# Four edits around the seams of a two-layer trunk: order of the expert stages' head, the last expert's rows by products, the tail LayerNorms on other engines

## The chip, the cores and the metric

The kernel runs on 1 core of one Trainium2 chip. The metric is the device time in microseconds (us) of one execution.

## The reference

A trunk of two layers over 512 tokens of width 1024, all in float32. Layer 0 mixes tokens by RWKV-7, layer 1 by forgetting attention (FoX). After each mixer comes a mixture of 16 experts with one router shared by both layers (top-1 group of four, in it top-2 experts). Each residual step is a LayerNorm with gain and shift:

```python
h = layer_norm(ALPHA * h + mixed, ln_g[i, 0], ln_b[i, 0])
ffn = shared_router_moe(h, router_w, router_bias, w_gate[i], w_up[i], w_down[i])
h = layer_norm(ALPHA * h + ffn, ln_g[i, 1], ln_b[i, 1])
```

For each token the experts give silu(x @ w_gate) * (x @ w_up) @ w_down, weighted by the two gates, which are scaled to a sum of one.

## The kernel before, in words

The stages run one after another: rwkv, moe for layer 0, fox (which begins with the LayerNorm that closes layer 0), moe for layer 1, and the last LayerNorm with the stores (trunk). Tokens lie in four tiles of 128. Products in full precision are made from two-part operands: ScalarE rounds a matrix to its high part (wsplitA, L200), VectorE subtracts to get the low part (wsplitB, L203), and three TensorE products (mm3, L68 to L70) add up.

Inside moe and between the stages the order on each engine is the order of the program text, and each engine takes its own queue in order. Inside rwkv, fox and the last LayerNorm a planner (Threads) interleaves generators: each yields estimated costs per engine, and the one whose time is least goes on; what it emits is again a fixed order on each engine.

*Head of an expert stage* (moe, from L193). From the router's sums VectorE works out the chosen experts in small operations (L209 to L231), TensorE counts positions, one-hot masks give the rows of the first expert, and GpSimd gathers them from the stored tokens hd (L253: 128 rows for experts 0 and 1; L262: half rows for the second block of up to 64 tokens). Then VectorE splits weight 0 (loA), works out codes, gate sums and the records of a table (L391 to L408) and the gate parts gp of expert 0 (L411 to L414), GpSimd scatters the table (L423), the tokens are transposed and split (xposeT, xposeS, xposeB; L280, L64, L65, L310), and VectorE splits weights 1 to 5. The first dense products are those of the second block (more(0), L314); in its middle a gate product (gates0, L419) needs gp, and VectorE copies its result (L420).

*Experts.* For each expert: more(e) if over 128 tokens chose it, then expert(e), which also splits the weights of the next one; each low part's subtraction lets SP load the weight eight places on. The expert's rows are added to the tokens zd in DRAM by an indirect DMA on GpSimd (scatter, L339). ORDER fixes which expert comes when. After the last expert there is a branch (L441) for experts with over 192 tokens.

*Closing LayerNorm* (Combine). It loads the sums z from zd (load_z, L467); in layer 0 the gain and shift rows are spread over the partitions by one-row products (spread, L462) and ScalarE copies (L465). For each tile ln_steps (L140): statistics, mean and variance on VectorE (L123 to L131), the square root and the normalisation on ScalarE (L126, L135), and gain and shift in halves on VectorE or GpSimd, whichever the planner has free sooner (L148). In the end each tile is stored whole (L1333).

*Tail of a mixer.* The last output products end in residual sums by halves (in fox L1254), the same ln_steps runs for each tile (After.norm), and the router transposes and multiplies the normalised tokens (L154, L159). Loads of the first weights start as buffers come free.

## Time and profile before

| | |
|---|---|
| time, median of 3 runs | 1638.11 us (1634.1 to 1641.88) |
| the profiled execution's own time | 1635.95 us |
| its span, first to last instruction | 1634.2 us |
| mean granted TensorE clock | 0.921 |
| TensorE busy | 1459.5 us (89%) |
| VectorE busy | 1163.1 us (71%) |
| ScalarE busy | 919.5 us (56%) |
| GpSimd busy | 530.7 us (32%) |

The profile names engines PE (TensorE products), PEld (its weight loads), DVE (VectorE), ACT (ScalarE), POOL (GpSimd) and SP (SyncE, which issues DMAs). L12 is line 12 of the kernel. A timeline row has start, duration, engine, line, operation, output and inputs by the program's names, shape and how many were merged; in brackets the idle time before and what ended it. A row of the windows view has the stretch, its length, the busy time and number of instructions that touch it for each engine, then the granted TensorE clock as a share of full speed, the DMA engines' busy share and GB/s.

### The profile page before, as it was taken

Reading aid. Unit: us, or ns where it says so; the run is one execution under the profiler, and the core shown is the slowest. Engines: PE = TensorE matmul, PEld = TensorE weight load, DVE = VectorE, ACT = ScalarE, POOL = GpSimd, SP = SyncE. Lnnn points to the kernel's source line nnn. Section 1 sums busy time; section 2 is a strip of 40 time slices with the busy share of each in tenths; the row PEclk is TensorE's granted clock in tenths of the full one; section 3 lists DMA queues with packets and bytes.
Section 4 is the critical chain, followed back from the end, with each engine's and each line's share of the span. In section 5 each row is a group of like instructions: output and inputs, shape, how many; then the busy total and the mean of one; then the engine's idle time right before and its main releaser. Section 6 shows DMA issues by size and latency. Waiting matters only on the chain. (4 is left out here: it accounts for less than half of the span.)

```text
span 1634.2 us, 24892 instructions
## 1 busy us (share of the span) xinstructions
PE 1459.5 (89%) x9125; PEld 1192.7 (73%) x9125; DVE 1163.1 (71%) x1873; ACT 919.5 (56%) x1355; POOL 530.7 (32%) x431
## 2 busy tenths in 40 slices
PE   6998977889976799999999699999885999999992
PEld 2587865887765688888887577777674888888881
DVE  7647779477585796887895637556647786968984
ACT  2553573534334486767885436545424786858872
POOL 4104785413242433322342323101104233313422
PEclk9998998587987899999999799999995999999996
DMA  7325532133345799897992424112427797979962
GB/s 221 123 84 187 162 99 83 27 98 117 111 142 189 239 331 316 287 358 232 357 344 94 157 72 123 37 61 72 155 104 227 244 364 247 358 249 346 350 204 106
DMA packets 202521, 313.61 MB, mean 192 GB/s; under 512 B 27914, under 2 KB 123490, under 8 KB 202356
## 3 DMA queue, kind: packets, MB, share of 16 engines
q1 hardware_dynamic: 178820, 267.74, 48.1%
q0 software_dynamic: 18816, 37.31, 8.0%
q10 hardware_dynamic: 4720, 6.44, 1.1%
q8 instruction: 93, 1.52, 0.4%
q14 instruction: 72, 0.59, 0.1%
HBM read 296.42 MB, written 41.75 MB: 207 GB/s over the span
## 5 line engine op out<-in xcount | busy, mean ns | idle before, releaser
L203 DVE TENSOR_TENSOR wl<-raw,wh 128x2048 fp32r<-128x2048 f32 (+1 forms) x168 | 334.7, 2006 | 5.9 <-DVEq L344 5.9
L200 ACT ACTIVATE wh<-raw 128x2048 fp32r<-128x2048 f32 (+1 forms) x168 | 282.7, 1688 | 15.7 <-ACT wh L200 9.0
L339 POOL DMA_INDIRECT zd<-yt,TB x38 | 113.7, 2992 | 432.2 <-ACT yt L306 386.0
L68 PE MATMUL bank<-wh,xm 128*128 128x256 f32 (+1 forms) x768 | 249.9, 325 | 3.9
L69 PE MATMUL bank<-wl,xm 128*128 128x256 f32 (+1 forms) x768 | 245.1, 319 | 0.0
L70 PE MATMUL bank<-wh,xm 128*128 128x256 f32 (+1 forms) x768 | 244.9, 319 | 0.0
L68 PEld LDWEIGHTS bank<-wh,xm 128*128 128x128 f32 x768 | 144.6, 188 | 26.0 <-issue 14.6
L69 PEld LDWEIGHTS bank<-wl,xm 128*128 128x128 f32 x768 | 144.7, 188 | 11.5
L70 PEld LDWEIGHTS bank<-wh,xm 128*128 128x128 f32 x768 | 144.6, 188 | 11.3
L203 DVE TENSOR_TENSOR wl<-rawo,wh 128x2048 fp32r<-128x2048 f32 (+1 forms) x56 | 110.2, 1980 | 24.9 <-ACT wh L200 24.4
L68 PE MATMUL bank<-wh,wh 128*128 128x512 f32 x256 | 111.5, 436 | 1.4 <-DVE kl L1169 0.8
L68 PE MATMUL bank<-wh,hm 128*128 128x512 f32 x256 | 111.3, 435 | 0.0
L70 PE MATMUL bank<-wh,wl 128*128 128x512 f32 x256 | 101.1, 395 | 3.6 <-DVE wl L1240 3.6
L70 PE MATMUL bank<-wh,hm 128*128 128x512 f32 x256 | 101.1, 395 | 0.0
L69 PE MATMUL bank<-wl,hm 128*128 128x512 f32 x256 | 100.8, 394 | 0.0
L200 ACT ACTIVATE wh<-rawo 128x2048 fp32r<-128x2048 f32 (+1 forms) x56 | 93.4, 1668 | 13.1 <-PE bank L70 9.0
L69 PE MATMUL bank<-wl,wh 128*128 128x512 f32 x256 | 100.6, 393 | 0.0
L1062 POOL TENSOR_TENSOR wl<-raw,wh 128x512 fp32r<-128x512 f32 x29 | 41.2, 1432 | 88.6 <-ACT wh L1061 87.0
L262 POOL DMA_INDIRECT xo<-hd,TB x30 | 61.1, 2037 | 11.9 <-issue 8.6
L64 ACT ACTIVATE xm<-bank 128x512 fp32r<-128x512 f32 x64 | 38.3, 598 | 42.5 <-PE bank L280 38.9
L68 PEld LDWEIGHTS bank<-wh,wh 128*128 128x128 f32 x256 | 49.2, 192 | 15.1 <-issue 6.0
L1197 ACT ACTIVATE sb<-sb,st 128x512 f32<-128x512 f32 (+1 forms) x64 | 35.8, 560 | 43.2 <-DVE st L1193 27.3
(531 smaller groups left out, 3504.1 us busy)
## 6 DMA issues: line engine op xcount, KB each, us to landing
raw<-in_moe_w_gate_dram SPq DMA_DIRECT2D x48, 1024.0 KB
raw<-in_moe_w_up_dram SPq DMA_DIRECT2D x48, 1024.0 KB
raw<-in_moe_w_down_dram SPq DMA_DIRECT2D x48, 1024.0 KB
rawo<-in_moe_w_up_dram SPq DMA_DIRECT2D x16, 1024.0 KB
rawo<-in_moe_w_down_dram SPq DMA_DIRECT2D x16, 1024.0 KB
rawo<-in_moe_w_gate_dram SPq DMA_DIRECT2D x14, 1024.0 KB
raw<-in_fx_w_in_dram SPq DMA_DIRECT2D x12, 1024.0 KB
raw<-in_rw_wk_dram SPq DMA_DIRECT2D x4, 1024.0 KB
```

The source lines that it names most:

```text
L64: nc.scalar.activation(hi,src,AF.Copy)
L68: nc.tensor.matmul(out,ah,bh,start=start,stop=False)
L69: nc.tensor.matmul(out,ah,bl,start=False,stop=False)
L70: nc.tensor.matmul(out,al,bh,start=False,stop=stop)
L200: Q=slice(None) if q is None else QS[q]; nc.scalar.activation(his[m%NH][:,Q],raws[m%NR][:,Q],AF.Copy)
L203: Q=slice(None) if q is None else QS[q]; V.tensor_tensor(los[m%NH][:,Q],raws[m%NR][:,Q],his[m%NH][:,Q].bitcast(F32),op=ALU.subtract)
L262: nc.gpsimd.indirect_dma_start(out=xo,out_offset=None,in_=hd.rearrange("t (h n) -> (t h) n",h=2), in_offset=bass.IndirectOffsetOnAxis(ap=T ...
L339: nc.gpsimd.indirect_dma_start(out=zd[:,:],out_offset=bass.IndirectOffsetOnAxis(ap=ix[0:n],axis=0), in_=y[0:n],in_offset=None,bounds_check ...
L1062: (V if d else G).tensor_tensor(lo[n][:,Q],raw[:,Q],hi[n][:,Q].bitcast(F32),op=ALU.subtract)
L1197: S.activation(SB[u][:,0:N],SB[u][:,0:N],AF.Exp,bias=ST[u][:,0:1],scale=-1.0,accum_out=ST[u][:,1:2])
```

## The change

- **Order of the head.** The codes go ahead of the split of weight 0; table records, code sums and gate sums go from VectorE to GpSimd as chains of small additions (total); a mask of the first choice (thr1) replaces the running sums of choices; the token transposes and all splits of weights come ahead of the gate parts gp. In layer 1 the first two weights are split in fox already (pre=2, t_early, the end of t_last).
- **The last expert's rows by products.** Expert 15 scatters nothing. z is loaded before it; a one-hot matrix hot of its rows against tokens is made, and after the branch Combine.sums adds, for each tile and half, identity times z and hot times the expert's output y in a PSUM bank: 16 products in fp32. The LayerNorm reads the banks. In layer 0 the gain and shift rows are spread inside expert 15.
- **LayerNorm.** ln_quick does everything but the square root on VectorE, two combined passes for each half. It is used for the last tile of both mixers and for tiles 2 and 3 of the last LayerNorm; tiles 0 and 1 there have gain and shift on GpSimd alone. The last stores are of half tiles.

```diff
+def ln_quick(C, th, z, i, out, gb, bb, mark, eps=LN_EPS, keys=()):
+    V=C.nc.vector; sm=C.sm[:,i%4]; N=(slice(0,512),slice(512,1024)); z=halves(z)
+    for n in range(2):
+        yield from th.need(*keys[n:n+1])
+        V.bn_stats(sm[:,6*n:6*n+6],z[n]); yield 'V',.69
+    V.bn_aggr(sm[:,12:14],sm[:,0:12].rearrange("p (a b) -> p a b",a=2))
+    V.tensor_scalar(sm[:,14:15],sm[:,13:14],eps,None,op0=ALU.add)
+    C.nc.scalar.activation(sm[:,15:16],sm[:,14:15],AF.Sqrt)
+    sub=lambda n: V.scalar_tensor_tensor(out[:,N[n]],z[n],sm[:,12:13],gb[:,N[n]],op0=ALU.subtract,op1=ALU.mult)
+    sub(0); V.reciprocal(sm[:,14:15],sm[:,15:16]); yield 'V',1.2
+    for n in range(2):
+        if n: sub(1)
+        V.scalar_tensor_tensor(out[:,N[n]],out[:,N[n]],sm[:,14:15],bb[:,N[n]],op0=ALU.mult,op1=ALU.add); yield 'V',.69*(n+1)
+        mark(n)
...
-        for m in range(NH): wsplitA(m)
+        for m in range(pre,NH): wsplitA(m)
...
+        G=nc.gpsimd; mk=su[:,384:512].rearrange("p (c t e) -> p c t e",c=2,e=NE); m0=mk[:,0].rearrange("p t (g e) -> p (t g) e",g=4)
+        V.tensor_tensor(m0,rk,C.thr1[:,None,:].to_broadcast([128,16,4]),op=ALU.is_lt)
+        G.tensor_tensor(m0,m0,gs.rearrange("p t g -> p (t g)")[:,:,None].to_broadcast([128,16,4]),op=ALU.mult)
+        G.tensor_tensor(mk[:,1],selb,mk[:,0],op=ALU.subtract)
...
         first(0)
+        mt=sTs[0].rearrange("p a b -> p (a b)").rearrange("p (c t e) -> p c t e",c=2,e=NE); red=p1.tile([128,3,8],F32,name="red"); idx=p1.tile([128,8],I32,name="idx")
+        mt2=sTs[1].rearrange("p a b -> p (a b)").rearrange("p (c t e) -> p c t e",c=2,e=NE)
+        ct=lambda t: t.rearrange("p c t e -> p (c t) e"); bc=lambda t: t[:,None,:,:].to_broadcast([128,2,NT,NE])
+        def total(out, t):
+            t=ct(t)
+            for n in (8,4,2): G.tensor_tensor(t[:,:,0:n],t[:,:,0:n],t[:,:,n:2*n],op=ALU.add)
+            G.tensor_tensor(out,t[:,:,0],t[:,:,1],op=ALU.add)
+        G.tensor_tensor(mt2,mk,bc(s),op=ALU.mult); total(red[:,1],mt2)
+        G.tensor_tensor(red[:,2,0:4],red[:,1,0:4],red[:,1,4:8],op=ALU.add)
...
-        loA(0); V.tensor_copy(sel,selb)
+        bl=su[:,256:320].rearrange("p (a b) -> p a b",b=NE); code=su[:,320:384].rearrange("p (a b) -> p a b",b=NE); pos=pp[:,0:NT,:]
+        V.tensor_scalar(bl,pos,127.5,None,op0=ALU.is_gt)
+        for n in (255.5,383.5): V.scalar_tensor_tensor(bl,pos,n,bl,op0=ALU.is_gt,op1=ALU.add)
+        V.scalar_tensor_tensor(code,pos,64.0,C.e4[:,None,:].to_broadcast([128,NT,NE]),op0=ALU.mult,op1=ALU.add)
+        V.scalar_tensor_tensor(code,bl,-8191.0,code,op0=ALU.mult,op1=ALU.add)
+        V.reciprocal(red[:,2,0:4],red[:,2,0:4]); V.tensor_scalar(red[:,2,0:4],red[:,2,0:4],1.0/ALPHA,None,op0=ALU.mult)
+        for m in range(pre): load(m+NR)
...
+            if not next_: comb.spread((pgo,tr[1]),0)
...
+            if not next_: comb.spread((pgo,tr[1]),2)
...
-            lo(4); dnA(w[5],5,1); outA(1,y,fo); scatter(src(e),y,128); hi(5); lo(5)
+            lo(4); dnA(w[5],5,1); outA(1,y,fo)
+            if next_: scatter(src(e),y,128)
+            hi(5); lo(5)
...
-        bl=su[:,256:320].rearrange("p (a b) -> p a b",b=NE); code=su[:,320:384].rearrange("p (a b) -> p a b",b=NE); pos=pp[:,0:NT,:]
-        V.tensor_scalar(bl,pos,127.5,None,op0=ALU.is_gt)
-        for n in (255.5,383.5): V.scalar_tensor_tensor(bl,pos,n,bl,op0=ALU.is_gt,op1=ALU.add)
-        V.scalar_tensor_tensor(code,pos,64.0,C.e4[:,None,:].to_broadcast([128,NT,NE]),op0=ALU.mult,op1=ALU.add)
-        V.scalar_tensor_tensor(code,bl,-8191.0,code,op0=ALU.mult,op1=ALU.add)
-        mk=su[:,384:512].rearrange("p (c t e) -> p c t e",c=2,e=NE); m1=mk[:,1].rearrange("p t (g e) -> p (t g) e",g=4)
-        V.memset(m1[:,:,0],0.0); V.tensor_copy(m1[:,:,1],selv[:,:,0])
-        V.tensor_tensor(m1[:,:,2],selv[:,:,0],selv[:,:,1],op=ALU.add)
-        V.tensor_tensor(m1[:,:,3],m1[:,:,2],selv[:,:,2],op=ALU.add)
-        V.tensor_tensor(mk[:,1],mk[:,1],sel,op=ALU.mult)
-        V.tensor_tensor(mk[:,0],sel,mk[:,1],op=ALU.subtract)
-        mt=sTs[0].rearrange("p a b -> p (a b)").rearrange("p (c t e) -> p c t e",c=2,e=NE); red=p1.tile([128,3,8],F32,name="red"); idx=p1.tile([128,8],I32,name="idx")
-        ct=lambda t: t.rearrange("p c t e -> p (c t) e"); bc=lambda t: t[:,None,:,:].to_broadcast([128,2,NT,NE])
-        V.tensor_tensor(mt,mk,bc(code),op=ALU.mult)
-        V.tensor_reduce(red[:,0,:,None],ct(mt),axis=AX.X,op=ALU.add); V.tensor_copy(idx,red[:,0])
-        V.tensor_tensor(mt,mk,bc(s),op=ALU.mult)
-        V.tensor_reduce(red[:,1,:,None],ct(mt),axis=AX.X,op=ALU.add)
-        V.tensor_tensor(red[:,2,0:4],red[:,1,0:4],red[:,1,4:8],op=ALU.add); V.reciprocal(red[:,2,0:4],red[:,2,0:4]); V.tensor_scalar(red[:,2,0:4],red[:,2,0:4],1.0/ALPHA,None,op0=ALU.mult)
-        V.tensor_tensor(C.rec[:,:,2].rearrange("p (c t) -> p c t",c=2).bitcast(F32),red[:,1].rearrange("p (c t) -> p c t",c=2),red[:,2:3,0:4].to_broadcast([128,2,NT]),op=ALU.mult)
+        if not pre: loA(0)
+        for hf in range(2): xposeT(xgs[0],hf,tr[hf]); xposeS(hf,tr[hf])
+        if not pre: loA(1)
+        xposeB()
+        for m in range(2,NH): loA(m)
+        G.tensor_tensor(mt,mk,bc(code),op=ALU.mult); total(red[:,0],mt)
+        G.tensor_copy(idx,red[:,0])
+        G.tensor_tensor(C.rec[:,:,2].rearrange("p (c t) -> p c t",c=2).bitcast(F32),red[:,1].rearrange("p (c t) -> p c t",c=2),red[:,2:3,0:4].to_broadcast([128,2,NT]),op=ALU.mult)
         g0=p1.tile([128,2],F32,name="g0"); gp=p1.tile([128,3,NT],BF16,name="gp"); gr=p1.tile([128,NT],F32,name="gr")
         V.tensor_tensor(gr,s[:,:,ORDER[0]],red[:,2,0:4],op=ALU.mult)
...
-        for hf in range(2): xposeT(xgs[0],hf,tr[hf]); xposeS(hf,tr[hf])
-        loA(1); xposeB()
-        for m in range(2,NH): loA(m)
         for e in range(NE):
             count(e+2)
             more(e)
             if e+2<NE or e==0: gather(src(2) if e==0 else src(e+2),xgs[e%2],128)
             if e+1<NE: gather2(e+1)
+            else:
+                comb.load_z(); hot,tok=xgs[0][:,0:512],xgs[0][:,512:1024]; me=p1.tile([128,1],F32,name="me")
+                nc.gpsimd.iota(tok,pattern=[[1,T]],base=0,channel_multiplier=0,allow_small_or_imprecise_dtypes=True)
+                V.tensor_copy(me,src(e)); V.tensor_scalar(hot,tok,me,None,op0=ALU.is_equal)
             expert(e)
         with tc.If(nc.values_load(most[0:1,0:1],min_val=0,max_val=T,skip_runtime_bounds_check_because="a count of 512 tokens")>192):
@@ -443,12 +475,14 @@
                 count(e)
                 for blk in (1,2,3):
                     with tc.If(rs[e]>max(192,128*blk)): rest(e,blk)
+            comb.load_z()
+        comb.sums(hot,ys[1])
...
+    def spread(s, banks, a):
+        if s.rows:
+            C=s.C
+            for n in (0,1): C.nc.tensor.matmul(banks[n],s.bb[0:1,896:1024],C.raws[3][0:1,(a+n)*512:(a+n+1)*512],start=True,stop=True)
+            for n in (0,1): C.nc.scalar.activation(C.raws[2][:,(a+n)*512:(a+n+1)*512],banks[n],AF.Copy)
...
+    def sums(s, hot, y):
+        for i in range(NT):
+            for n in range(2):
+                N=slice(n*512,(n+1)*512); mm=s.C.nc.tensor.matmul
+                mm(s.C.bk[2*i+n],s.C.ident,s.h[i][:,N],start=True,stop=False,skip_group_check=True)
+                mm(s.C.bk[2*i+n],hot[:,i*128:(i+1)*128],y[:,N],start=False,stop=True,skip_group_check=True)
...
+    def steps(s, i, th, how='', mark=lambda n: None):
+        C=s.C; z,out=C.bk[2*i:2*i+2],s.h[i]
+        if how=='Q': yield from ln_quick(C,th,z,i,out,s.gb,s.bb,mark,eps=LN_EPS/ALPHA**2); return
+        if how=='G':
+            ln_stats(C,z,i,LN_EPS/ALPHA**2); ln_scale(C,i); yield 'V',2.0
+            ln_norm(C,z,i,out); yield 's',1.6
+            for n in range(2):
+                N=slice(n*512,(n+1)*512); G=C.nc.gpsimd
+                G.tensor_tensor(out[:,N],out[:,N],s.gb[:,N],op=ALU.mult); G.tensor_tensor(out[:,N],out[:,N],s.bb[:,N],op=ALU.add); mark(n)
+            return
+        yield from ln_steps(s.C,th,s.C.bk[2*i:2*i+2],i,s.h[i],s.gb,s.bb,eps=LN_EPS/ALPHA**2)
...
-    comb.load_z(); comb.spread(); comb.spread2()
...
+        if i<NT-1: yield from need(f"r{i}0",f"r{i}1")
+        yield from after.norm(i,z[i],th,z[i],(f"r{i}0",f"r{i}1"))
+        if i==NT-1: after.lo(0,1); after.lo(1)
+    def t_early():
+        yield from need(f"r{NT-1}0")
+        yield .8
+        after.hi(0,0); yield 'S',.95
+        after.lo(0,0); yield 'v',1.15
+        after.hi(0,1); after.hi(1); yield 'S',2.9
...
+        if i==NT-1: yield from ln_quick(s.C,th,z,i,out,s.gb,s.bb,mark,keys=keys)
+        else: yield from ln_steps(s.C,th,z,i,out,s.gb,s.bb,mark)
...
-        moe(C,1,W,hd[1],zd[1],load[1],0)
-        cb[1].load_z()
+        moe(C,1,W,hd[1],zd[1],cb[1],load[1],0,pre=2)
         th=Threads()
         def last(i):
-            yield 2.0*i
-            yield from cb[1].steps(i,th)
-            nc.sync.dma_start(out[0,i*128:(i+1)*128,:],cb[1].h[i])
+            yield 2.1*i
+            N=lambda n: slice(n*512,(n+1)*512)
+            yield from cb[1].steps(i,th,'GGQQ'[i],lambda n: nc.sync.dma_start(out[0,i*128:(i+1)*128,N(n)],cb[1].h[i][:,N(n)]))
```

## Rows read from the trace of the kernel before

**Rows 1.** The page's head, busy time of each engine over the span.
```profile
PE 1459.5 (89%) x9125; PEld 1192.7 (73%) x9125; DVE 1163.1 (71%) x1873; ACT 919.5 (56%) x1355; POOL 530.7 (32%) x431
```

**Rows 2.** Windows view, a stretch inside the second expert stage.
```profile
1550.00:1602.00 52.00, 51.70 (x310) 44.60 (x308) 38.18 (x36) 32.51 (x36) 14.32 (x6) 1.00 0.54 177
```

**Rows 3.** Timeline, the last tile's LayerNorm at the end of fox.
```profile
1221.09 1.28 DVE L123 BATCH_NORM_STATS2 sm<-raw 128x6 f32<-128x512 f32 x2
...
1224.31 2.75 DVE L148 TENSOR_TENSOR raw<-raw,raw 128x512 f32<-128x512 f32 x4 [0.88 <-ACT raw L135]
...
1225.78 1.11 PE L154 MATMUL bank<-ident,raw 128*128 128x128 f32 x4 [5.33 <-DVE raw L148]
```

**Rows 4.** Timeline, the head of layer 0's expert stage.
```profile
530.54 2.29 DVE L203 TENSOR_TENSOR wl<-raw,wh 128x2048 fp32r<-128x2048 f32 x1
...
535.36 0.60 ACT L64 ACTIVATE xm<-bank 128x512 fp32r<-128x512 f32 x1 [2.53 <-DMA rawo<-in_moe_w_gate_dram]
...
537.02 0.15 DVE L411 TENSOR_TENSOR gr<-s,red 128x4 f32<-128x4 f32 x1
...
538.09 1.28 DVE L65 TENSOR_TENSOR xm<-bank,xm 128x512 fp32r<-128x512 f32 x2
...
542.01 0.77 PE L314 MATMUL bank<-wh,xh 128*128 128x512 f32 x1 [2.06 <-issue]
...
542.71 8.95 DVE L203 TENSOR_TENSOR wl<-raw,wh 128x2048 fp32r<-128x2048 f32 x4
...
547.71 0.45 PE L419 MATMUL bank<-gp,yt 128*128 128x1 bf16 x12
```

**Rows 5.** Windows view, the stretches in which the clock rose, both heads.
```profile
546.00:547.00 1.00, 1.00 (x5) 0.84 (x4) 1.00 (x1) 0.00 (x0) 0.79 (x1) 0.91 0.92 118
...
1259.00:1260.00 1.00, 1.00 (x5) 0.76 (x3) 1.00 (x1) 0.00 (x0) 0.78 (x1) 0.72 0.97 242
```

**Rows 6.** Timeline, the head of layer 1's expert stage.
```profile
1253.71 0.76 PE L314 MATMUL bank<-wh,xh 128*128 128x512 f32 x1 [2.11 <-DVE xh L65]
...
1254.38 8.95 DVE L203 TENSOR_TENSOR wl<-raw,wh 128x2048 fp32r<-128x2048 f32 x4
...
1260.17 0.45 PE L419 MATMUL bank<-gp,yt 128*128 128x1 bf16 x12
```

**Rows 7.** Timeline, a small operation on GpSimd at the start of fox.
```profile
898.72 0.28 POOL L1035 CAST idb<-ident 128x128 bf16<-128x128 f32 x1
```

**Rows 8.** Timeline, from the last expert of layer 0 into fox.
```profile
889.77 0.60 ACT L306 ACTIVATE yt<-bank 128x512 f32<-128x512 f32 x1 [0.80 <-PE bank L70]
...
892.85 5.75 PE L462 MATMUL bank<-raw,raw 1*128 1x512 f32 x8 [3.12 <-ACTq L441]
...
896.93 0.60 ACT L465 ACTIVATE raw<-bank 128x512 f32<-128x512 f32 x1 [1.11 <-PE bank L462]
...
898.64 0.60 ACT L465 ACTIVATE raw<-bank 128x512 f32<-128x512 f32 x1 [1.11 <-PE bank L462]
...
901.05 1.29 DVE L123 BATCH_NORM_STATS2 sm<-raw 128x6 f32<-128x512 f32 x2 [14.63 <-DMA raw<-zd]
...
914.59 3.45 PE L1051 MATMUL bank<-ident,raw 128*128 128x128 f32 x12 [2.48 <-DVE raw L148]
...
917.70 0.72 PE L68 MATMUL bank<-wh,wh 128*128 128x512 f32 x1
```

**Rows 9.** Windows view with TensorE alone, the same seam.
```profile
897.50:898.00 0.50, 0.50 (x2) 0.50 0.00 0
...
918.00:918.50 0.50, 0.50 (x4) 0.77 0.00 0
```

**Rows 10.** Timeline, after the last expert of layer 1.
```profile
1605.38 1.28 ACT L126 ACT_TABLE_LOAD   x1 [2.75 <-ACTq L441]
...
1617.46 1.74 DVE L148 TENSOR_TENSOR raw<-raw,raw 128x512 f32<-128x512 f32 x1
...
1623.62 6.70 DVE L148 TENSOR_TENSOR raw<-raw,raw 128x512 f32<-128x512 f32 x9
```

More of the change, by code (lines that the diff above doesn't have):

```diff
@@ L175, in place, with moe @@
     queue.dma_start(raw.rearrange("p (k n) -> p k n",k=kk),(M[:,hf*n:(hf+1)*n] if w==1 else M[hf*128*kk:(hf+1)*128*kk,:]).rearrange("(k p) n -> p k n",p=128))
-def moe(C, L, W, hd, zd, load, tail, late=()):
+def moe(C, L, W, hd, zd, comb, load, tail, late=(), pre=0):
     nc,tc=C.nc,C.tc; V=nc.vector
@@ L1014, in fox_vload @@
     C.nc.sync.dma_start(k4(dst),P['win'][k*512:(k+1)*512,2048+n*512:2048+(n+1)*512].rearrange("(k p) n -> p k n",p=128))
[L1016 removed]
+FX_SCHED=(0,.5,-1,0,0,2,4,6,15)+(0,)*17
 def fox(C, comb, P, after):
@@ L1256, in t_last @@
     def t_last(i):
-        yield from need(f"r{i}0",f"r{i}1")
-        yield from after.norm(i,z[i],th,z[i])
+        if i<NT-1: yield from need(f"r{i}0",f"r{i}1")
[7 more added lines that the diff above has]
+        after.hi(0,1); after.hi(1); yield 'S',2.9
     def t_route():
@@ L1265, in fox @@
     for i in range(NT): th.add(t_tokens(i))
-    for g,bi in zip((t_values(0),t_wv(),t_gates(),t_values(1),t_weights(),t_qk(),t_post(0),t_post(1),t_score(),t_soft(),t_norm(),t_transpose(),t_av(),t_oparts(),t_oproj(0),t_oproj(1),*[t_last(i) for i in range(NT)],t_route()),
-                    (*bias,*[0]*8)): th.add(g,bi)
+    for g,bi in zip((t_values(0),t_wv(),t_gates(),t_values(1),t_weights(),t_qk(),t_post(0),t_post(1),t_score(),t_soft(),t_norm(),t_transpose(),t_av(),t_oparts(),t_oproj(0),t_oproj(1),*[t_last(i) for i in range(NT)],t_early(),t_route()),
+                    (*bias,*[0]*9)): th.add(g,bi)
     th.run()
@@ L1275, in free, with norm @@
     def free(s, n): s.load(n)
-    def norm(s, i, z, th, out):
-        yield from ln_steps(s.C,th,z,i,out,s.gb,s.bb,lambda n: th.done.add(f"y{i}{n}"))
+    def norm(s, i, z, th, out, keys=()):
+        mark=lambda n: th.done.add(f"y{i}{n}")
+        if i==NT-1: yield from ln_quick(s.C,th,z,i,out,s.gb,s.bb,mark,keys=keys)
+        else: yield from ln_steps(s.C,th,z,i,out,s.gb,s.bb,mark)
         (s.C.nc.sync if i==NT-1 else s.C.nc.gpsimd).dma_start(s.hd[i*128:(i+1)*128,:],out)
```

23 lines of the change are left out of this document (9 added, 14 removed).

## The prediction

> **What bounds the kernel now.** I read the page's head first, then busy time and clock by stage, then the timeline at the four places that the diff touches: both heads of the expert stages, the seam from the first expert stage to FoX, and the end. TensorE is busy for 89% of the span [rows 1], and inside an expert stage for 51.7 of 52 us at full clock [rows 2]. So work of VectorE, ScalarE or GpSimd that is moved inside the stages is worth nothing by itself, while a shift of a whole stage's start carries through to the end. What can be won or lost lies where TensorE waits: from the router's sum to the first dense products of a stage, between the stages, and after the last product. The profiled execution took 1635.95 us (span 1634.2 and 1.75 around it), 2.2 below the median of 1638.11; the sum is made against 1635.95.
>
> **The last tile's LayerNorm in front of a stage.** Today 4.69 us pass from the first statistics to the first router transpose [rows 3]. ln_quick drops ScalarE's pass and one small operation and needs statistics (1.28), three small operations (about 0.2 each) and two passes of 0.7 (2.75 for four) for the first half: 3.3, so 1.3 us earlier in layer 0. In layer 1 the first half's statistics are taken before the last product ends: 1.8 earlier. The splits of the first two weights that go into this gap (t_early) stand behind data that came long before and beside idle engines; their cost is nothing, and at most one 1.2 us pass of VectorE if they come late.
>
> **Head of layer 0.** Read the VectorE queue [rows 4]. Its small operations between the split of weight 0 (over at 532.8) and the second halves of the tokens (538.09) take 5.3 us; the change keeps about 1.5 of them, in front of that split, and gives the rest to GpSimd. The token halves then wait for ScalarE (535.36 plus 0.60) instead: start 535.5, 2.6 earlier. The first product moves from 542.0 to 539.4, and the splits of weights 2 to 5 (8.95 us in one piece) run from 540.1 to 549.1. But the gate parts gp, six small operations (537.02 to 538.09), stood ahead of all this and now stand behind the fifth split in the program, and VectorE takes its queue in order: gp is there at 550.2. TensorE needs it for the gate product L419, after 5.7 us of products (542.01 to 547.71). It comes there at 545.1 and now waits 5 us; today it doesn't wait. The gate product goes from 547.7 to 550.3: 2.6 us **lost** where 2.6 seemed won. Everything behind it on TensorE's queue (the rest of the second block, then expert 0) waits with it, and the stage is bound by TensorE.
>
> A wait of 5 us also costs clock. After such pauses the dense products began at 542.01 and 1253.71 and the granted clock rose in the stretches 546 to 547 and 1259 to 1260 [rows 5, 6]: about 4 and 6 us at half speed, so 2 to 3 us lost; I take 2.3, with 0 as the lower end. Sum of this head: **+4.9**, between +2.6 and +8.
>
> The GpSimd work: two masks ahead of the first gather, six small operations behind it (each 0.3 to 0.5 by the cast of 0.28 [rows 7]), so the half-row gather and the second gather issue some 2 us later; the token halves cover the first. Seven more stand before the table scatters, which begin about when they do now. If that cover is gone, the half rows are late for the first product by up to 2 us, but VectorE's gate parts are later still. Of VectorE's new operations only the thr1 mask (0.2) lies on the chain to the gather.
>
> **Head of layer 1.** Same order, 1.8 earlier, without weights 0 and 1 on VectorE. The first product could start at about 1247 instead of 1253.7, the 8.95 us of splits run 1248 to 1257, gp comes at 1258.2, the gate product at 1258.3 instead of 1260.17: **-1.9**. But TensorE stands still from about 1253.6, where today it runs through and has just been given full clock (L419 follows on without a pause): plus 2.3 for the clock. Sum **+0.4**, between -1.9 and +3. Of the 6.7 us by which the first product starts earlier, nothing arrives: VectorE's splits are the longer chain.
>
> **From layer 0 to FoX.** Removed: the scatter of the last expert, the wait for it and the load of z (out of expert 15 at 889.77, first statistics at 901.05 [rows 8]). Added in expert 15 of layer 0: four one-row products that spread the LayerNorm's rows. They show 1.71 us apart at half clock (their copies at 896.93 and 898.64), so 0.86 at full clock and 3.4 in all, on TensorE's path; today they are hidden in the wait. Their ScalarE copies (0.60 each) lie beside products. The z load is issued one expert earlier behind the scatter of expert 14, on SP ahead of FoX's loads; some 15 us of products cover it. The branch keeps its price: from the last eviction at 889.77 to TensorE's next product 892.85, 3.1 us. Then come 16 products in fp32 of 512 columns, 0.86 each as the one-row ones: 13.7 at full clock. The 3.1 us pause lets the clock fall as it fell today (0.50 at 897.5 [rows 9]), plus 2.3: 16.0. So tile 0 is complete at about 902, against 901.05 now, and tile 3 at 892.85 + 3.4 + 16.0 = 912.2. The tokens' transposes stand behind all of this in TensorE's queue; today the last twelve of them begin at 914.59, and the first FoX product follows at 917.70. The tiles now come 4 us apart, about as fast as the LayerNorms take them, so the lateness of 1 us at the first tile grows little: 1 to 4 us at the first FoX product, I take **+2.5**; the ends are -1 (full clock throughout) and +14 (below).
>
> **The end.** TensorE's products start after the branch at 1605.4, where ScalarE's table load stands today [rows 10]; 16.0 us later, at 1621.4, the last tile is complete, tile 2 at 1618.0. Tile 2 and 3 then need on VectorE alone 8.7 us (three halves' statistics 1.9, eight passes 5.6, six small ones 1.2): 1626.7. Beside GpSimd a pass took 1.74, where nine in a row took 6.70 or 0.74 each; GpSimd is at its eight operations of 1.3 or more until about 1625, so one or two passes are stretched: 1627.8. The last pass ends today at 1630.3, and the last store is half as long: **-2.5**, between -5 (no clock lost) and +9 (below).
>
> Sum: 4.9 + 0.4 + 2.5 - 2.5 = **+5.3 us**, 1641.3 against the profiled execution's own time and 1643.4 against the median; I put the middle, **1642.4**. The smallest difference a measurement of this kernel tells from none is about 0.5%, 8.2 us, so the forecast is no change that can be told, on the slow side.
>
> **Rivals.**
> 1. *The fp32 products stay at half clock to their end* (slower). For: the one-row products kept TensorE busy from 892.85 to 898.6, and the clock was still 0.50 at the end. Against: the fp32 transposes from 914.59 on were followed by full clock at 918 [rows 8, 9]. Price: 27.3 instead of 16.0 at each place, +11.3, or +22.6 at both: 1654 to 1665. It decides when the clock row in the last third of the products still shows 0.50. Chance 0.12. The Trainium skill (TensorE: Matmul & The Clock Gate, the part on the warm-up) says that activity of the array releases the throttle and that the idle state is the slow one. By it the products would bring the clock back and the sum above stands; the rows at 897.5, busy and still slow, don't agree with it for one-row products.
> 2. *The gate parts are not held back* (faster): VectorE's queue gives gp before the splits, the change's early starts come through, -2.6 and -6.5 at the heads, without lost clock: 1635.95 - 9.1 + 2.5 - 2.5 = 1626.9. For: the first product really is freed by some microseconds in both heads. Against: all VectorE rows of today's head stand in the program's order. Chance 0.10.
> 3. *No clock is lost anywhere* and the sums take 13.7: +2.6 - 1.9 - 1 - 5 = -5.3, 1630.6. Against: the pauses of 3.1 us and more in these rows were followed by half clock. Chance 0.15.
> 4. *GpSimd's small operations are held up by VectorE's splits*, so gathers and table come late: up to 2.3 each for some of the 13; the half rows and the table's first users have 2 to 3 us of cover. Price some +4: 1646. For: two engines' passes stretched each other [rows 10]. Chance 0.13.
>
> **How the numbers follow.** The forecast keeps 0.50, with own range 1635 to 1651 from the ends of its four terms taken together. The range of 1630 to 1657 reaches to rival 3 below and to one place of rival 1 above; left out are rival 2 and both places of rival 1. Faster by over 0.5%: rival 2 and half of 3, 0.17. Slower by over 0.5%: rival 1, half of 4, and the upper two fifths of the forecast, 0.38. The rest, 0.45, within.
>
> **What would show it.** In the changed trace: the gate product L419's place waits some 5 us for a DVE cast in both heads, with the clock row falling to 0.50 behind it; the first products of the heads 2.6 and 6.5 us earlier, expert 0 not earlier in layer 0; 16 products of 0.86 or 1.71 between the branch and each LayerNorm; no scatter after the last eviction. The prediction is wrong if the gate product waits for nothing, if the clock stays full, or if the last third of the products is still at half.

## The result, and the profile after

The changed kernel takes **1650.69 us** (median of 7 runs, 1646.07 to 1653.06), the kernel before 1638.11 over the runs made beside it: ratio **1.0087**, 95% interval 1.0067 to 1.0107. It is slower by more than the 0.5% that can be told. The range of 1630 to 1657 held it; the likeliest figure (1642.4, no change that can be told) was 8 us short.

The profiled execution took 1653.06 us (span 1651.0), so the two traces differ by 16.8 us where the medians differ by 12.6. The page's busy line of the changed kernel answers to [rows 1]: TensorE is busy for 39 us more. 31 of these are the sums by products, which stand in large part where TensorE stood idle before. Most of the rest is half clock in the two heads and slower products in the experts; the one-row products were there before too (5.75 us busy then, 3.93 now).

```profile
PE 1498.4 (91%) x9189; PEld 1211.5 (73%) x9189; DVE 1157.7 (70%) x1846; ACT 913.1 (55%) x1348; POOL 541.5 (33%) x464
```

To find the place, I cut both spans at the same instructions (the router's sigmoid, the weight load of the first dense product of the second block, its gate product, expert 0's and expert 15's first Silu on ScalarE, the last eviction of expert 15, FoX's first eviction) and subtract; the forecast's terms stand beside.

| stretch, us | before | after | difference | forecast |
|---|---|---|---|---|
| start to sigmoid, layer 0 | 519.38 | 518.27 | -1.1 | -1.3 |
| sigmoid to first dense product | 22.60 | 20.47 | -2.1 | -1.3 |
| first dense product to gate product | 5.74 | 9.96 | +4.2 | +5.2 |
| gate product to expert 0's Silu | 18.04 | 22.19 | +4.2 | +2.3 |
| expert 0's Silu to expert 15's | 312.28 | 313.96 | +1.7 | 0 |
| that to the last eviction | 11.74 | 17.68 | +5.9 | +3.4 |
| to FoX's first eviction | 34.95 | 35.14 | +0.2 | -0.9 |
| to sigmoid, layer 1 | 306.78 | 305.87 | -0.9 | -1.8 |
| sigmoid to first dense product | 22.19 | 19.36 | -2.8 | -4.9 |
| first dense product to gate product | 6.49 | 9.91 | +3.4 | +4.8 |
| gate product to expert 0's Silu | 17.94 | 23.12 | +5.2 | +2.3 |
| expert 0's Silu to expert 15's | 312.18 | 314.41 | +2.2 | 0 |
| that to the last eviction | 11.74 | 11.81 | +0.1 | 0 |
| to the end | 32.19 | 28.89 | -3.3 | -2.5 |

The first stretch has no weight: among the profiles below it ran from 510.6 to 521.2, though their code differs from the changed kernel's only behind it (and by one small constant in runs 3, 7 and 11). All lengths below are of the stretches after it. They vary too where the code is the same: the end took 27.0 to 30.1 in nine profiles besides the changed kernel's, and gate product to Silu 22.2 to 23.5 in the heads that no run had repaired.

**Head of layer 0.** Timeline of the changed kernel, answering to [rows 4]:

```profile
538.77 0.77 PE L351 MATMUL bank<-wh,xh 128*128 128x512 f32 x1 [2.26 <-issue]
...
539.48 8.89 DVE L219 TENSOR_TENSOR wl<-raw,wh 128x2048 fp32r<-128x2048 f32 x4
...
548.47 0.17 DVE L443 CAST gp<-gr 128x4 bf16<-128x4 f32 x1
...
548.70 0.16 PE L449 MATMUL bank<-gp,yt 128*128 128x1 bf16 x1 [3.50 <-DVE gp L443]
...
556.89 1.28 ACT L365 ACT_TABLE_LOAD   x1 [11.06 <-PE bank L363]
...
559.50 0.50 PE L351 MATMUL bank<-wh,hs 128*128 128x512 f32 x1 [1.79 <-DVE hs L65]
```

The forecast's wait is there: TensorE stands for 3.50 us until gp comes from behind the splits. The last two rows are not in the forecast: a table load (ACT_TABLE_LOAD, which stands ahead of the Silu) on ScalarE that waits for TensorE, and TensorE waiting for what comes out behind it. The windows view with TensorE alone shows half clock behind the first pause (stretch, length, busy, clock, DMA share, GB/s):

```profile
546.00:547.00 1.00, 0.00 (x0) 1.00 0.99 387
547.00:548.00 1.00, 0.00 (x0) 0.78 1.00 394
...
553.00:554.00 1.00, 1.00 (x7) 0.50 1.05 401
554.00:555.00 1.00, 1.00 (x9) 0.80 0.90 338
```

**Head of layer 1.** The timeline again, against [rows 6]:

```profile
1254.36 1.08 POOL L293 DMA_INDIRECT xo<-hd,i  x1 [0.51 <-issue]
1254.53 0.99 SPq L191 DMA_DIRECT2D raw<-in_moe_w_up_dram  x2
...
1260.80 1.09 PE L347 MATMUL bank<-ident,xo 128*128 128x128 f32 x4 [3.58 <-DMA xo<-hd,i]
...
1262.36 0.43 DVE L65 TENSOR_TENSOR xh<-bank,xh 128x256 fp32r<-128x256 f32 x1 [3.77 <-ACT xh L64]
...
1262.93 0.76 PE L351 MATMUL bank<-wh,xh 128*128 128x512 f32 x1 [1.04 <-DVE xh L65]
...
1263.58 8.89 DVE L219 TENSOR_TENSOR wl<-raw,wh 128x2048 fp32r<-128x2048 f32 x4
...
1272.81 0.16 PE L449 MATMUL bank<-gp,yt 128*128 128x1 bf16 x1 [3.70 <-DVE gp L443]
```

Here the gather of the half rows, behind six GpSimd operations, sets the first dense product. VectorE stands for 3.77 us until it can split the half rows, and the splits of the weights and gp follow behind that in its queue; the gp wait follows as in layer 0.

**Expert 15 of layer 0.** Timeline, then the windows view with all engines (busy of TensorE, its weight loads, VectorE, ScalarE, GpSimd, then clock, DMA share, GB/s):

```profile
884.88 1.95 PE L498 MATMUL bank<-raw,raw 1*128 1x512 f32 x4
...
889.83 1.98 PE L498 MATMUL bank<-raw,raw 1*128 1x512 f32 x4
```

```profile
891.00:892.00 1.00, 1.00 (x4) 0.26 (x3) 1.00 (x1) 0.74 (x2) 0.00 (x0) 1.00 0.76 225
892.00:893.00 1.00, 1.00 (x8) 1.00 (x8) 0.69 (x1) 0.45 (x1) 0.00 (x0) 0.66 0.94 332
...
894.00:895.00 1.00, 1.00 (x6) 1.00 (x6) 0.00 (x0) 0.00 (x0) 0.00 (x0) 0.50 0.36 147
```

TensorE is busy in every one of these rows, and the clock falls all the same.

**The end** (timeline, against [rows 10]): the products start 3.1 us after the last eviction and tile 3 is complete 15.7 us later, for which 16.0 was forecast. The last two rows are of the windows view with TensorE alone: the clock is back at 1.00 from 1630 on.

```profile
1622.15 0.60 ACT L343 ACTIVATE yt<-bank 128x512 f32<-128x512 f32 x1 [0.80 <-PE bank L70]
1625.26 1.20 PE L505 MATMUL bank<-raw,ident 128*128 128x512 f32 x2 [3.15 <-ACTq L473]
...
1633.41 10.76 POOL L518 TENSOR_TENSOR raw<-raw,raw 128x512 f32<-128x512 f32 x8 [23.32 <-ACT raw L135]
...
1639.93 1.02 PE L506 MATMUL bank<-yt,xg 128*128 128x512 f32 x2
...
1647.26 0.75 DVE L165 SCALAR_TENSOR_TENSOR raw<-raw,sm,raw 128x512 f32<-128x512 f32 x1
```

```profile
1628.00:1629.00 1.00, 1.00 (x3) 0.50 0.00 0
...
1630.00:1631.00 1.00, 1.00 (x4) 1.00 0.00 0
```

### The profile page after: what moved, and what is told of

Read it like the earlier page. It is cut to its first block, busy times and chain, and to the rows that moved or that the text cites. A ratio compares the mean times of both kernels' runs of the same rounds, so it can differ in the third digit from the quotient of the medians.

```text
span 1651.0 us, 25030 instructions
## 1 busy us (share of the span) xinstructions
PE 1498.4 (91%) x9189; PEld 1211.5 (73%) x9189; DVE 1157.7 (70%) x1846; ACT 913.1 (55%) x1348; POOL 541.5 (33%) x464
## 5 line engine op out<-in xcount | busy, mean ns | idle before, releaser
L219 DVE TENSOR_TENSOR wl<-raw,wh 128x2048 fp32r<-128x2048 f32 (+1 forms) x166 | 329.9, 2001 | 5.4 <-DVEq L381 5.4
L216 ACT ACTIVATE wh<-raw 128x2048 fp32r<-128x2048 f32 (+1 forms) x166 | 279.3, 1686 | 19.6 <-ACT wh L216 9.5
L219 DVE TENSOR_TENSOR wl<-rawo,wh 128x2048 fp32r<-128x2048 f32 (+1 forms) x56 | 110.2, 1980 | 23.1 <-ACT wh L216 22.6
L70 PEld LDWEIGHTS bank<-wh,wl 128*128 128x128 f32 x256 | 48.9, 191 | 15.7 <-DVE wl L1289 4.9
```

The lines of the kernel that those rows point to most:

```text
L70: nc.tensor.matmul(out,al,bh,start=False,stop=stop)
L216: Q=slice(None) if q is None else QS[q]; nc.scalar.activation(his[m%NH][:,Q],raws[m%NR][:,Q],AF.Copy)
L219: Q=slice(None) if q is None else QS[q]; V.tensor_tensor(los[m%NH][:,Q],raws[m%NR][:,Q],his[m%NH][:,Q].bitcast(F32),op=ALU.subtract)
```

## The experiments

All are edits of the changed kernel unless said otherwise; ratios are to the kernel before, run beside them. The first four each follow one suspicion, separately.

**1. Gate parts ahead of the splits.**

```diff
+        V.tensor_tensor(gr,s[:,:,ORDER[0]],red[:,2,0:4],op=ALU.mult)
+        for c in range(3):
+            V.tensor_copy(gp[:,c],gr)
+            if c<2: V.tensor_tensor(gr,gr,gp[:,c],op=ALU.subtract)
         for m in range(pre): load(m+NR)
...
-        V.tensor_tensor(gr,s[:,:,ORDER[0]],red[:,2,0:4],op=ALU.mult)
-        for c in range(3):
-            V.tensor_copy(gp[:,c],gr)
-            if c<2: V.tensor_tensor(gr,gr,gp[:,c],op=ALU.subtract)
```

> One edit to the changed kernel: the gate parts gp (six small VectorE operations) stand ahead of the weight splits again, right behind the gate sums. Theory (the heads lose because gp stands behind 8.9 us of splits in VectorE's queue): the gate product waits less than 0.5 us in both heads (now 3.50 and 3.70), its twelve products take 0.45 instead of 1.4, the granted clock stays at 1.00 behind it. Layer 0: minus 3.5 for the pause, 1.0 for the chain, 1.9 for the half clock, plus 1.0 because six operations now stand before the first splits: expert 0's first activation, now 5.1 later than in the kernel before, comes 5.4 earlier. Layer 1: minus 3.7, 1.0, 1.8, and nothing added, as VectorE has 3.8 us idle there: 6.5 earlier. Whole kernel about 12 us faster than the changed one, about 1639. Rival (the heads lose on the side of the gathers and the table, or by the new silu wait, whatever the order of gp): the pause only moves to the next product that needs those, each head gains under 2 us, the whole about 1647 to 1650.

Measured 1642.56 us, ratio 1.0041 (1.0016 to 1.0065). The pause is gone in both heads, the twelve small products take 0.45, and from sigmoid to expert 0's Silu the heads take 47.4 and 45.3 us (52.6 and 52.4 in the changed kernel): 5.2 and 7.1 gained, where 5.4 and 6.5 were expected. The medians moved less, by 0.46% or 7.6 us; the profiled execution, 1635.84, was among the fastest of this kernel. What is left shows next in the timeline of this run:

```profile
541.30 0.45 PE L449 MATMUL bank<-gp,yt 128*128 128x1 bf16 x12
...
546.85 1.28 ACT L370 ACT_TABLE_LOAD   x1 [4.75 <-PE bank L368]
...
549.47 0.55 PE L356 MATMUL bank<-wh,hs 128*128 128x512 f32 x1 [1.79 <-DVE hs L65]
```

```profile
548.00:549.00 1.00, 0.00 (x0) 1.00 1.03 391
549.00:550.00 1.00, 0.54 (x2) 0.89 1.05 405
550.00:551.00 1.00, 1.00 (x4) 0.50 1.04 401
```

So the clock now falls behind the second pause, the one of the table load: gate product to Silu is still 21.1 and 20.6 against 18.0 before. The theory holds; the rival named a real second wait.

**2. No pause, same wait.**

```diff
                 if e==0:
+                    for _ in range(15): nc.tensor.matmul(pum,Xh[:,0].rearrange("p t c -> p (t c)"),k4(w[0][0])[:,0],start=True,stop=True)
                     gates0(1)
```

> One edit to the changed kernel: ahead of the gate product of the second block TensorE does 15 products of 128x512 whose results are thrown away (about 3.5 us at full clock), in both heads, so that it does not stand still there; nothing of the result changes. This prices the clock by itself: the gate product must still come when gp is there (548.7 and 1272.8). Theory (a pause costs twice, once itself and once by half clock after it): the granted clock stays at 1.00 behind the gate product, expert 0 comes 1.9 earlier in layer 0 and 1.8 to 3.3 earlier in layer 1 (where the clock fell a second time), about 4 to 5 in all. Rival (the clock falls for another reason than the pause, or the gap through the twelve small products is enough): clock at 0.50 behind the gate product as now, and no gain, or up to 1 us of loss.

Measured 1644.55, ratio 1.0055 (1.0039 to 1.0072). The gate product comes no earlier after the sigmoid (30.2 us against 30.4), but the clock stays:

```profile
539.36 3.66 PE L384 MATMUL bank<-wh,xh 128*128 128x512 f32 x15
...
543.59 0.16 PE L451 MATMUL bank<-gp,yt 128*128 128x1 bf16 x1 [0.56 <-DVE gp L445]
```

```profile
544.00:545.00 1.00, 0.61 (x12) 1.00 0.69 231
545.00:546.00 1.00, 1.00 (x10) 1.00 0.97 342
```

Gate product to Silu: 20.2 instead of 22.2, and 21.3 instead of 23.1. So a pause of 3.5 us cost about 2 us of clock on top of itself (1 to 3 by the spread of the unrepaired heads, 22.2 to 23.5): the forecast's 2.3 was right in size. In layer 1 the clock still fell behind the table load's pause, so the upper end of 3.3 was not reached.

**3. Buffers at their old addresses.**

```diff
-        V.tensor_tensor(m0,rk,C.thr1[:,None,:].to_broadcast([128,16,4]),op=ALU.is_lt)
+        V.scalar_tensor_tensor(m0,rk,1.0,C.thr[:,None,:].to_broadcast([128,16,4]),op0=ALU.add,op1=ALU.is_lt)
...
-me=p1.tile([128,1],F32,name="me")
+me=i2.bitcast(F32)
```

> Two edits to the changed kernel that leave all work where it is but allocate no new buffer: the threshold of the first choice is taken from the old one with the add inside the comparison, and the index of the last expert's rows goes into a buffer that exists. So every later buffer lies at its address of the kernel before. Theory (the steady growth of 0.11 us for each expert, 1.7 in layer 0 and 2.2 in layer 1, comes from where the operands lie: the 256-column products start 119.9 ns apart on the mean where they started 118.5 apart): the spacing goes back to 118.5, expert 15's first activation is then as far behind the kernel before as expert 0's, within 0.3 in layer 0, and 0.6 in layer 1 (a step of 0.5 at expert 1 may stay); about 3.5 us faster. Rival (the growth comes from code, queues or the clock): it stays at 0.10 to 0.12 for each expert, and the time is that of the changed kernel within 1.

Expert 0's Silu to expert 15's takes 312.46 and 312.91 (changed 313.96 and 314.41; before 312.28 and 312.18): the growth is gone but for the step at expert 1 of layer 1. Over all of layer 0's experts the starts of neighbouring 256-column products lie 120.33 ns apart before, 121.61 in the changed kernel, 120.33 here (mean of some 740 differences each; the 118.5 and 119.9 of the expectation leave out the gaps). The whole gained less, 1648.85, ratio 1.0085 (1.0058 to 1.0111): in its profiled execution 1.1 us went in the head of layer 0, where the clock fell a second time, behind the table load's pause, and 1.1 at the end. That the addresses matter is shown by the stretches, not by the medians.

**4. The LayerNorm's rows by DMA, no one-row products.**

```diff
-            if k==2: cb[0].ones()
-            if k==3: cb[0].load_gb1()
+            if k==2: cb[0].load_gb()
```

> One edit to the changed kernel: the gain and shift rows of layer 0's closing LayerNorm are read spread over the partitions by DMA while the last expert runs (as layer 1's already are), so the four one-row products in expert 15 and their copies go. Theory (these products cost 3.9 us by themselves and 2.0 more because the granted clock fell to 0.50 behind them, 892 to 895): the clock stays at 1.00 to the end of expert 15, the last eviction of layer 0 comes 5.9 earlier, the stages behind it keep their lengths, about 5.5 faster in all. Rival (the one-row products lay beside other waits, or the 1 MB of rows is late and holds up the LayerNorm or FoX's loads): under 2 us, or slower by what the loads come late, up to 3.

Measured 1645.70, ratio 1.0061 (1.0040 to 1.0083). Expert 15's Silu to the last eviction: 11.81, 5.9 less, as expected. From there to FoX's first eviction it takes 36.97 instead of 35.14, 1.8 back, so some of the rival is true too. The trace places it at the branch behind the last expert (L473): TensorE's first sum product starts 5.78 us after the last eviction, against 3.17 in the changed kernel. In all three kernels with the rows by DMA (runs 4, 7 and 11) this takes 5.6 to 5.8, in the others 3.0 to 3.7. What holds the branch longer stays open. The rows of the changed kernel and of this run (timelines):

```profile
905.71 1.80 PE L505 MATMUL bank<-raw,ident 128*128 128x512 f32 x2 [3.21 <-ACTq L473]
...
901.24 2.08 PE L505 MATMUL bank<-raw,ident 128*128 128x512 f32 x2 [5.81 <-ACTq L473]
```

**5. The table load.** From here on edits are added up. The first Silu waits for TensorE and VectorE; in the changed kernel it waits for a third engine too, GpSimd, which uses the small tiles that this Silu writes. In the trace ScalarE's wait for TensorE then stands in an instruction of its own ahead of the table load. The edit gives GpSimd other tiles.

```diff
-        mt=sTs[0].rearrange("p a b -> p (a b)").rearrange("p (c t e) -> p c t e",c=2,e=NE)
-        mt2=sTs[1].rearrange("p a b -> p (a b)").rearrange("p (c t e) -> p c t e",c=2,e=NE)
+        mt=ys[0][:,0:128].rearrange("p (c t e) -> p c t e",c=2,e=NE)
+        mt2=ys[0][:,128:256].rearrange("p (c t e) -> p c t e",c=2,e=NE)
```

> Edits to the changed kernel: the gate parts early as in the first run, and GpSimd's two scratch tiles for the gate sums and codes lie in the first output buffer instead of in the two small tiles that the second block's Silu writes. Theory (ScalarE's first Silu now has a third engine to wait for, GpSimd, so its wait for TensorE stands in an instruction of its own ahead of the table load; the load of 1.28 us no longer lies beside the products but behind them, TensorE waits 1.8 us and the clock falls after that): with another scratch the table load is issued right behind the copy of the second block's first bank, as in the kernel before, and from the gate product to expert 0's Silu it takes 18.0 in both heads (before 18.04 and 17.94; with the gate parts early alone 21.1 and 20.6): 5.7 us better than that run. Rival (the table load is late because ScalarE comes to it late, or the clock falls for another reason): 21 and 20.6 as there, and no gain.

Measured 1631.13, ratio 0.9984 (0.9968 to 1.0001). The wait ahead of the load is over in 17 ns, where one of 11627 ns stood in the changed kernel (the Silu's line in both, durations in ns, least, median and most):

```profile
L365 ACTq EVENT_SEMAPHORE  x6: 4602/4604/11627, 545.2 to 1461.0; - x6
...
L370 ACTq EVENT_SEMAPHORE  x6: 17/17/17, 540.3 to 1438.4; - x6
```

The load is back behind the copy, beside products, and the Silu follows TensorE at once:

```profile
540.27 0.60 ACT L387 ACTIVATE xo<-bank 128x512 f32<-128x512 f32 x1 [5.07 <-PE bank L356]
540.88 1.28 ACT L370 ACT_TABLE_LOAD   x1
...
545.87 0.28 ACT L370 ACTIVATE sT<-bank 128x128 f32<-128x128 f32 x1 [3.70 <-PE bank L368]
```

Gate product to Silu: 18.5 and 17.6. The rival falls. The load's duration of 1.28 is the one that the Trainium skill gives for the load by itself (ScalarE: Activation LUTs, What ACT_TABLE_LOAD costs); what it costs here is not its duration but where its wait stands: 1.79 us of TensorE, then clock.

**6. The half rows first.**

```diff
-        G.tensor_tensor(mt2,mk,bc(s),op=ALU.mult); total(red[:,1],mt2)
-        G.tensor_tensor(red[:,2,0:4],red[:,1,0:4],red[:,1,4:8],op=ALU.add)
...
         gather2(0)
+        G.tensor_tensor(mt2,mk,bc(s),op=ALU.mult); total(red[:,1],mt2)
+        G.tensor_tensor(red[:,2,0:4],red[:,1,0:4],red[:,1,4:8],op=ALU.add)
```

> The kernel of the run before with one more edit: GpSimd issues the gather of the half rows ahead of its six operations on the gate sums instead of behind them. Theory (in layer 1 the first dense product waits for the half rows, whose gather is issued 1.9 us later than in the kernel before because of these operations): the gather is issued 2 us earlier and lands before the two weight loads of 1 MB that go out 0.2 us behind it today; from the router's sigmoid to the first dense product layer 1 takes 17.2 to 15.5 instead of 19.1; layer 0, where VectorE's second split stands in front of the half rows anyway, stays at 20.3 to 20.8. Between 2 and 3.5 us faster than the run before. Rival (the half rows land when the DMA engines are done with what was queued before, whenever the gather is issued): layer 1 stays within 0.5 of 19.1, or gets slower, as the gate sums now come later.

Measured 1629.16, ratio 0.9970 (0.9950 to 0.9991). Layer 1's sigmoid to first dense product is 16.2 instead of 19.6, layer 0's 20.4 instead of 20.8: as the theory has it. 1.2 of it is given back at expert 1 of layer 1 (experts 315.6 instead of 314.4), where TensorE waits 1.0 us for expert 1's half rows, whose index comes out of the table. The whole times of runs 5 and 6 can't be told apart.

**7. All five.** The edits of runs 3 and 4 on top of run 6, among them:

```diff
-            if k==2: cb[0].ones()
-            if k==3: cb[0].load_gb1()
+            if k==2: cb[0].load_gb()
...
-me=p1.tile([128,1],F32,name="me")
+me=i2.bitcast(F32)
```

> All five edits together: gate parts early, other scratch, half rows first, buffers at their old addresses, the rows of layer 0's LayerNorm by DMA. If the terms are separate they add up: against the changed kernel 5.2 and 7.1 (gate parts), 3.1 and 2.6 (Silu's wait), 2 to 3.5 (half rows, layer 1), 1.5 and 1.5 (addresses), 5.9 less 1.8 (the seam to FoX was 36.97 with the rows by DMA, 35.14 without): 27 to 29 faster, about 1622 against 1650.7 of the changed kernel and 1637 of the one before. Rival (a shared bound, VectorE's splits in the heads or the loads behind the seam, takes some of it back): 1628 to 1635. It is also the version that may beat both kernels.

Measured **1624.49** (1617.83 to 1626.34), ratio **0.9930** (0.9903 to 0.9957): faster than both kernels. From layer 0's sigmoid to the end the stretches add up to 1103.2 us, against 1132.8 in the changed kernel and 1114.8 before: 29.6 of 27 to 29 expected. Of these, 28.5 lie in the stretches that the edits touch (heads 7.7 and 12.5, experts 2.9, expert 15 to FoX 5.4); the end, which none touches, gave 1.9, and FoX lost 0.9. So the terms add up. The medians moved by 26.2.

**8. The old head, with products and LayerNorms new.** The changed kernel with the lines of the head, t_early and the early splits undone:

```diff
-        if not pre: loA(0)
-        for hf in range(2): xposeT(xgs[0],hf,tr[hf]); xposeS(hf,tr[hf])
-        if not pre: loA(1)
-        xposeB()
-        for m in range(2,NH): loA(m)
...
+        loA(0); V.tensor_copy(sel,selb)
...
+        for hf in range(2): xposeT(xgs[0],hf,tr[hf]); xposeS(hf,tr[hf])
+        loA(1); xposeB()
+        for m in range(2,NH): loA(m)
```

> The changed kernel with the head of both expert stages in the order of the kernel before; the last expert's rows by products and the new LayerNorms stay (the one new constant too, so the buffers stay shifted). It splits the change in two. Theory (all of the loss in the heads comes from their new order, and the products and LayerNorms alone lose in expert 15 what they win at the end): the heads take 46.4 and 46.6 from the sigmoid to expert 0's Silu, as before (changed kernel 52.6 and 52.4); expert 15 of layer 0 stays 5.9 longer, the end 3.3 shorter, the growth of 0.1 for each expert stays: about 5 slower than the kernel before, ratio 1.003. Rival (the growth comes with the head's order, or the table's smaller cover): expert stages without growth, 1 to 2 slower than the kernel before.

Measured 1636.92, ratio 1.0027 (1.0005 to 1.0048), as expected. The heads take 46.9 and 46.1; the experts still grow (313.92, 313.91), so the growth does not come with the head. Expert 15 took only 16.2: the one-row products were there, but here the clock did not fall.

```profile
877.00:878.00 1.00, 1.00 (x4) 1.00 1.03 406
878.00:879.00 1.00, 1.00 (x7) 1.00 1.02 389
```

**9. All rows of the array.**

```diff
-            for n in (0,1): C.nc.tensor.matmul(banks[n],s.bb[0:1,896:1024],C.raws[3][0:1,(a+n)*512:(a+n+1)*512],start=True,stop=True)
+            for n in (0,1): C.nc.tensor.matmul(banks[n],C.ident,C.raws[3][:,(a+n)*512:(a+n+1)*512],start=True,stop=True)
```

> The changed kernel with the four one-row products of expert 15 replaced by four products of the same 512 fp32 columns over all 128 rows (identity times the whole row buffer). It leaves out the spreading: layer 0's closing LayerNorm gets other gain and shift values, so the output is another; the time of each product should be the same. Theory (one row of the array at work counts as little: the profile has TensorE busy all through, and the granted clock fell to 0.50 behind them in this kernel and in five of the six variants that have them): the four products still take 3.9 to 4.5 in all, the clock stays at 1.00 through expert 15, and from its Silu to the last eviction it takes 15.7 to 16.3 instead of 17.7 (11.7 without them). Rival (the fall comes with fp32 products or with the small waits around them, however many rows): clock at 0.50 behind them again, 17.6.

This kernel ran once. With other rows in that LayerNorm the second layer's router chooses otherwise, so the whole time (1813.81) says nothing; the stretch in question does. The products take 1.95 and 1.88 for each two (1.95 and 1.98 with one row), the clock stays full, and Silu to last eviction is 15.6:

```profile
891.93 1.88 PE L498 MATMUL bank<-raw,ident 128*128 128x512 f32 x4
```

```profile
892.00:893.00 1.00, 1.00 (x4) 1.00 1.02 406
893.00:894.00 1.00, 1.00 (x5) 1.00 0.97 348
```

With run 8 this makes the price of the one-row products 4.4 without and 5.9 with the fall, which came in seven of the eight profiled kernels that have them. As the clock stayed up once with one row too (run 8), one execution with all rows is consistent with the theory and does not show it.

**10. The old last LayerNorm on the new sums.**

```diff
-            yield from cb[1].steps(i,th,'GGQQ'[i],lambda n: nc.sync.dma_start(out[0,i*128:(i+1)*128,N(n)],cb[1].h[i][:,N(n)]))
+            yield from cb[1].steps(i,th)
+            nc.sync.dma_start(out[0,i*128:(i+1)*128,:],cb[1].h[i])
```

> The changed kernel with the last LayerNorm as before (shared between VectorE and GpSimd by the planner, whole tiles stored), on the sums that the products leave in the banks. It splits the gain of 3.3 us at the end. Theory (most of it is the scatter, its wait and the load of z that went; the last tile's own work is much the same, on VectorE alone or shared): from the last eviction to the end 28.9 becomes 29 to 30. Rival (the LayerNorm by tiles and the half stores bring it): 31 to 32.2, as in the kernel before.

It ran once, in 1650.04 us. From the last eviction to the end it takes 31.06, against 28.89 in the changed kernel and 32.19 before: the rival is nearer. By these figures the LayerNorm and the half stores bring 2.2 and the products 1.1; but with the same code the end took 27.0 to 30.1 in other profiles, so the split is rough. ScalarE's passes and the shared order came back behind the last sum:

```profile
1637.18 2.78 ACT L135 ACTIVATE raw<-bank,sm 128x512 f32<-128x512 f32 x4
...
1637.38 6.71 DVE L148 TENSOR_TENSOR raw<-raw,raw 128x512 f32<-128x512 f32 x9
```

**11. Half rows ahead of weight 1's split, in layer 0.** On top of the five edits:

```diff
-        if not pre: loA(1)
         xposeB()
+        if not pre: loA(1)
```

> The kernel with all five edits and one more: in layer 0 the half rows are transposed and split ahead of the low part of weight 1 on VectorE, not behind it (layer 1, where that split was done in FoX, is untouched). From the trace of the five edits: the half rows' halves would start at 540.0 instead of 541.3, the first dense product 1.4 earlier, weight 1's low part is there 0.8 before its first product. Theory (VectorE's 2.3 us split is what holds up the first product): sigmoid to first product 19.1 instead of 20.6 in layer 0, and expert 0's Silu 1.0 to 1.4 earlier; about 1623. Rival (TensorE then waits for weight 1's or weight 2's low part, or the clock stays low longer): no gain up to the Silu.

Measured 1626.29, ratio 0.9956 (0.9940 to 0.9971): no gain. The outcome is the rival's, though by another wait than those that it names. The first dense product does come 1.4 us earlier after the sigmoid (19.2), but five splits now stand in one piece, and the copy of the gate product's result behind them:

```profile
543.01 0.15 DVE L450 COPY g<-bank 128x1 f32<-128x1 f32 x1
543.26 0.88 DVE L364 TENSOR_SCALAR su<-bank,g 128x256 f32<-128x256 f32 x2
543.80 0.66 PE L368 MATMUL bank<-pair,su 128*128 128x64 f32 x4 [2.61 <-DVE su L364]
```

TensorE waits 2.61 us for it, the clock falls, and gate product to Silu is 23.3 instead of 17.9: the changed kernel's fault once more, one instruction further on.

## Why the prediction was right or wrong

**Right:** the central step. VectorE's queue holds gp back, TensorE waits at the gate product in both heads, the earlier first products come to nothing, and the pause is paid again in clock (runs 1 and 2). The head of layer 0 came out at +5.1 against +4.9, by luck: the terms were off on both sides, the wait shorter and something new behind it. The sums by products (15.7 against 16.0), the seam and the end (-3.3 against -2.5) were right within 1.1 us. Rival 1 did not come (the sums are at full clock from their fourth product on, in both layers), nor did rivals 2 and 3. Of rival 4 the effect came in layer 1, half rows that are late, but by the operations ahead of them in GpSimd's own queue (run 6).

That the range held is luck in part: its upper end, 1657, was drawn for rival 1, which did not come, and terms put at nothing filled it instead.

**Wrong:** the sum was 11.5 us short against the trace (16.8 for 5.3). Of this, 4.5 lie in the head of layer 1 (+4.9 for +0.4), 3.9 in the experts, 2.5 in expert 15 and 1.1 in the seam behind it, in these steps.

- *"The gate product goes from 547.7 to 550.3 ... plus 2.3 for the clock"* closes the head there. Behind it the Silu's table load had lost its cover: 1.79 us of waiting, and more half clock behind it in layer 1. Gate product to Silu cost +4.2 and +5.2 for +2.3 each. I costed the operations given to GpSimd by duration and start, and did not ask what else their scratch tiles are used for. Run 5 gave back 2.6 and 3.0 of run 1's times.
- *"0.86 at full clock and 3.4 in all"* for the one-row products was too small (1.95 and 1.98 for two, where 1.71 was counted, and about 0.5 of gaps around them) and left out the clock: 4.4 to 5.9. Rival 1 had the very row [rows 9] that showed one-row products busy at half clock, and I used it only for the sums. The Trainium skill's rule (TensorE: Matmul & The Clock Gate, Part 1), that activity releases the throttle, was weighed there against that row; in expert 15 the row was right in seven of eight profiles.
- *"The first product could start at about 1247"*, 4.9 earlier than the LayerNorm alone makes it: it was 2.8. Of the half rows the forecast says "the token halves cover the first"; that held in layer 0 only, where weight 1's split stands between. In layer 1 that split had gone to FoX and the cover with it. For that case the forecast had "VectorE's gate parts are later still", but the splits and gp stand behind the half rows in VectorE's queue and came later with them (VectorE idle for 3.77 us).
- *Work inside the stages costed at nothing*: the new constant of 16 bytes and the index of 4 in each partition moved the buffers behind them, and from expert to expert 0.11 us came on top, 3.9 us over both layers with the step at expert 1; 3.0 of it went with the old addresses (run 3).

The chances are thus the second fault: with costs left at nothing that could only grow, slower deserved more than 0.38.

## What to carry to other kernels

When an engine takes its queue in order, price a moved block by the small operations that now stand behind it, up to the last one that another engine waits for, and do so again after each repair: gp and, in run 11, the gate copy were two of the same kind. A wait of TensorE of 2 to 4 us in these heads was paid once itself and, by differences between runs, some 1 to 3 us again in clock (2.0 and 1.8 in run 2, 2.7 in run 11). And before an operation changes engines, look who else writes its scratch: a third engine in front of an instruction can move that instruction's wait ahead of the work that used to hide it.

## What the hardware showed that was not expected

- Behind four one-row products in a busy stretch the granted clock fell from 1.00 to 0.50 (from 892 on in the changed kernel), with TensorE busy at 1.00 all the while, in seven of eight profiled kernels. In the eighth (run 8), and in the one execution with 128 rows and about equal durations (run 9), it stayed at 1.00; that the rows are the cause is not shown.
- The pace of products depends on where the buffers lie: 121.61 against 120.33 ns for 256 columns and, gaps left out, 233.2 against 232.3 for 512, after a shift by a few bytes (which of the two new buffers did it was not tried). At the old addresses it was 120.33 and 232.6 (run 3).
- The Silu's table load of 1.28 us stood behind a separate instruction that waited for TensorE where the Silu had to wait for three engines, and ahead of that wait where it had to wait for two (8.2 us behind the gate product in the changed kernel, 0.8 in run 5). Whether the number of engines decides it in general was not tried.
- GpSimd's product on 128x128 took 2.21 us beside a split of VectorE (531.54 and 531.15 in the changed kernel, the split 2.29 us long) and 0.47 without one. No wait of TensorE in that head names it.
